# A two-step norm of queries and keys, stores on another queue, and a moved output-gate pair in a hybrid decoder layer

## The chip, the cores and the metric

The kernel runs on one core of a Trainium2 chip. The core has TensorE (PE, matmuls; its weight loads are listed as PEld), VectorE (DVE), ScalarE (ACT), GpSimd (POOL) and SyncE (SP), each with an instruction queue of its own that is worked in order, and 16 DMA engines. The metric is the device time of one execution in microseconds (us); lower is better.

## What is computed

One decoder layer, sequence 1024, width 1024, in float32: a half-step SwiGLU feed-forward, a token mixer, and a second half-step feed-forward, each behind an RMS norm with a shift and a scale. The change lies in the mixer's input projections. Cut to them:

```python
u = h @ w_in
da_q, da_k, da_v, ml_qk, ml_v, ml_o, ml_i, ml_f = jnp.split(u, IN_SPLITS, axis=-1)
q = partial_rope(rmsnorm(da_q per 64 channels, g_qnorm), cos, sin)   # and k likewise
y_da = diff_attention(q, k, da_v, ...)
ml_qk = silu(causal_conv(ml_qk, conv_w, conv_b))                     # 4 taps
y_ml = mlstm(ml_q, ml_k, ml_v, ml_o, ...)                            # gated by sigmoid(ml_o)
return concatenate([y_da, y_ml]) @ w_out
```

## The kernel before

All activations lie transposed, channels on the 128 partitions, 512 positions (half the sequence) on the free axis. A large projection is done by pairs of 128-channel output tiles. For each pair `wino` (line 226) computes the two tiles over both halves of the sequence with seven products in place of eight (Strassen's scheme): the activations' quarters and their differences are named B11, B21, B22 and T1 to T4, and the weight sums are formed in `wsum`. A product is four blocks of three matmuls (`mm3`, lines 199 to 201), because every float32 operand is split into a rounded part and a rest. For each product `split_w` (lines 187, 188) casts a weight block on ScalarE and takes the rest on VectorE. Results are added on VectorE (line 229).

A planner orders the instructions of each engine when the kernel is built: it simulates the engines and takes, by the order of the program, what is ready in its simulation. Buffers of a pool are handed out in the order of the program, and an instruction that writes into a reused buffer waits for the last use of the old one, a store included. `keep_in_program_order`, which the change uses, fixes an instruction's place.

The mixer's projections run in this order: values of attention (`wdv`, two pairs), gates, first mLSTM value pair (`wmv` 0), four pairs of queries and keys (`wqk`, `qk_handlers`), second mLSTM value pair (`wmv` 1), four pairs for the convolutions (`wcv`, `conv_handlers`), two pairs of output gates (`wmo`, `o_handlers`). Then mLSTM and attention heads follow.

What is left to do for a pair is put into `L.pending` and called by `late` in a later pair, behind its product T1. That holds for the transposes of values (line 642) and for `qk_finish` (line 591). `qk_finish` is called once for the queries and once for the keys: eight small matmuls sum the squares of each group of 64 channels (line 598), VectorE takes the reciprocal root (lines 601, 602), ScalarE spreads it into a tile `c` per half of the sequence (line 605), four matmuls turn that tile (line 609), ScalarE copies it back (line 611), and `qk_turned` scales, rotates and splits the four tiles of that half (lines 614 to 631). Each split tile is stored to DRAM in two parts (`qkd`, line 631, SP's queue). The raw tiles lie in eight buffers `qraw`, the casts in three buffers `qhi`. The queries and keys are in the pool `qkp`; when it closes, the convolutions' pool `cvp` takes the same memory, so the first write into `cu` (memset, line 726, or copy, line 746) waits for the last store out of `qkp`.

Other stores of the mixer, all on SP's queue: attention values (line 1136), mLSTM values (1141), convolved queries and keys (739), gates (758). GpSimd's queue carries attention's loads (lines 765 to 772). The first mLSTM head's loads stand on ScalarE's queue (lines 859 to 861); the buffer of the third lies where the gates' tiles lay.

Of the kernel before, what the change touches and what calls it, by code (L numbers as in the profile page):

```python
# [25 lines left out]
P = 128  # L26
# [104 lines left out]
HALF = [slice(0, HT), slice(HT, T)]  # L131


class Layer:
    def __init__(self, tc, A, es):
        self.tc, self.nc, self.A, self.es = tc, tc.nc, A, es
        nc = self.nc
        pool = lambda name, **k: es.enter_context(tc.tile_pool(name=name, **k))
        self.const = pool("const", bufs=1)
        c = self.const  # L140
        self.ones = c.tile([P, 1], F32, name="ones")
        nc.vector.memset(self.ones, 1.0)
        self.eps = c.tile([P, 1], F32, name="eps")
        nc.vector.memset(self.eps, EPS)
        self.mod = c.tile([P, 72], F32, name="mod")
        self.G = c.tile([P, 24], F32, name="G")
        self.gate = c.tile([P, 24], F32, name="gate")
        self.bada = c.tile([P, 72], F32, name="bada")
        self.gn = c.tile([P, 24], F32, name="gn")
        self.cs = c.tile([P, KT], F32, name="cs")  # L150
        self.B, self.full = {}, {}
        self.nct = 3
        self.sums = nc.gpsimd
        self.pending = []

    def ps(self):
        return self.mmps.tile([P, HT], F32, tag="mm", name="mm")
# [4 lines left out]
    def late(self):  # L162

        p, self.pending = self.pending, []
        for f in p:
            f()

# [58 lines left out]
    def wino(self, src, got11, out, got, st=None):  # L226
# [6 lines left out]
        if st is None:  # L233
# [18 lines left out]
            c22 = out("22")  # L252
            add(c22, w, y7)
            self.prod(z3, self.split_w(self.wsum(a12, s2, ALU.subtract)), "B22", True)
        else:
            p1 = st["p1"]
            s1 = self.wsum(a21, a22, ALU.add)
# [333 lines left out]
    def qk_finish(self, which):  # L591

        nc = self.nc
        ps = self.ps()
        for hf in range(2):
            for i in range(4):
                c = 8 * (4 * hf + i)
                nc.tensor.matmul(ps[:, c:c + 8], self.accs[which][hf][:, i * P:(i + 1) * P], self.bd[:, 0:P:16],
                                 start=True, stop=True, skip_group_check=True)
        v, y, t = (self.qkp.tile([P, 64], F32, tag=f"qn{i}", name=f"qn{i}") for i in range(3))  # L600
        nc.vector.tensor_scalar(out=v, in0=ps[:, 0:64], scalar1=1.0 / 64, scalar2=EPS, op0=ALU.mult, op1=ALU.add)
        self.rsqrt(y, t, v)
        for hf in range(2):
            r = self.ct()
            nc.scalar.copy(out=r.rearrange("p (c d) -> p c d", d=16),
                           in_=y[:, 32 * hf:32 * hf + 32].unsqueeze(2).broadcast_to([P, 32, 16]))
            ps = self.ps()
            for i in range(4):
                nc.tensor.matmul(ps[:, i * P:(i + 1) * P], r[:, i * P:(i + 1) * P], self.ident,
                                 start=True, stop=True, skip_group_check=True)  # L610
            nc.scalar.copy(out=r, in_=ps)
            self.qk_turned(which, hf, r)

    def qk_turned(self, which, hf, r):
        nc = self.nc
        hs = HALF[hf]
        for t in range(4):
# [10 lines left out]
            nc.scalar.copy(out=hi, in_=x)  # L628
            nc.vector.tensor_tensor(out=x, in0=x, in1=hi.bitcast(F32), op=ALU.subtract)
            for part, src in ((0, hi.bitcast(F32)), (1, x)):  # L630
                nc.sync.dma_start(out=self.qkd[which][:, part, 16 * t:16 * t + 16, hs], in_=src)


    def v_handlers(self, store):
# [85 lines left out]
    def conv_handlers(self, h):  # L720
# [2 lines left out]
        us = []  # L723
        for i in range(2):
            u = self.cvp.tile([P, T + 3], F32, tag="cu", name="cu", bufs=4)
            nc.gpsimd.memset(u[:, 0:3], 0.0)
            us.append(u)
        place = {"12": (0, 1), "21": (1, 0), "22": (1, 1)}
        at = lambda e, hf: us[e][:, 3 + hf * HT:3 + (hf + 1) * HT]
# [1 line left out]
        def conv(e):  # L731
# [4 lines left out]
            for j in range(1, 4):  # L736
                nc.vector.scalar_tensor_tensor(out=v, in0=u[:, j:j + T], scalar=cw(j), in1=v, op0=ALU.mult, op1=ALU.add)
            nc.scalar.activation(out=v, in_=v, func=AF.Silu)
            nc.sync.dma_start(out=self.mlqk[i], in_=v)

        def got(n, c):
            if n == "12":
# [5 lines left out]
    def o_handlers(self, pr):  # L748

        nc = self.nc  # L750
        t = lambda n=None: self.mle.tile([P, HT], F32, tag="vc", name="vc", bufs=6)
        place = {"12": (0, 1), "21": (1, 0), "22": (1, 1)}

        def fin(e, hf, src, v):
            h = 2 * pr + e
            nc.scalar.activation(out=v, in_=src, func=AF.Tanh, scale=0.5)
            nc.vector.tensor_scalar(out=v, in0=v, scalar1=1.0, scalar2=self.ghalf[:, h:h + 1], op0=ALU.add, op1=ALU.mult)
            nc.sync.dma_start(out=self.mlo[h][:, HALF[hf]], in_=v)
        return (lambda x: fin(0, 0, x, t())), t, lambda n, c: fin(*place[n], c, c)


# [210 lines left out]
def build(tc, yT, **A):  # L972
    nc = tc.nc
    with ExitStack() as es:
# [158 lines left out]

        def dav_store(pr):
            def store(e, hf, v):
                nc.sync.dma_start(out=davd[:, 4 * hf:4 * hf + 4, 2 * pr + e, :], in_=v)
            return store

        def mlv_store(pr):
            def store(e, hf, v):  # L1140
                nc.sync.dma_start(out=L.mlv[2 * pr + e][:, 4 * hf:4 * hf + 4, :], in_=v)
            return store
        dvh = [L.v_handlers(dav_store(pr)) for pr in range(2)]
        starts = [L.wino_p1(A["wdv"][i]) for i in range(2)]
# [63 lines left out]
        for which in range(2):  # L1208
# [11 lines left out]
                    L.wino(A["wqk"][i], seen11, out, got)  # L1220
            L.pending.append(lambda w=which: L.qk_finish(w))
        L.wino(A["wmv"][1], *L.v_handlers(mlv_store(1)))
        pq.close()

        pq, qpool = stack("right")
        L.cvp = qpool("cvp", bufs=2)
        for h in range(4):
            L.wino(A["wcv"][h], *L.conv_handlers(h))
        for pr in range(2):
            L.wino(A["wmo"][pr], *L.o_handlers(pr))  # L1230
        pq.close()
        pm.close()
        pt.close()
# [132 lines left out]
```

## Time and profile before

| | us |
|---|---|
| median of 3 runs | 2032.3 |
| lowest and highest | 2028.05, 2034.02 |
| profiled execution | 2026.9 |
| its span, first to last instruction | 2025.1 |
| PE busy in the span | 1919.7 (95%) |
| DVE busy | 1472.3 (73%) |
| ACT busy | 775.0 (38%) |
| POOL busy | 279.5 (14%) |

The first feed-forward fills the span until about 700 us, the mixer's projections lie between about 740 and 1082 us, mLSTM and attention between 1082 and 1220, the output projection and the second feed-forward behind. In the profile a time in brackets behind an instruction is the time for which its engine stood idle ahead of it, with what ended that. PEclk is the granted clock of TensorE as a share of its full 2.4 GHz; 0.50 is the lower level, 1.2 GHz. Busy times of neighbouring instructions overlap a little.

### The profile page before, as it was taken

To read this page: it belongs to the slowest core of one execution; us is meant where nothing else is said; L and a number is where in the kernel's file an instruction comes from. 1 tells how busy PE (TensorE), PEld (TensorE's weight loads), DVE (VectorE), ACT (ScalarE), POOL (GpSimd) and SP (SyncE) were. 2 spreads that over 40 slices of the span, in tenths; PEclk is the share of its full clock that TensorE was granted. 3 is DMA by queue.
4 is the path that set the end of the run, shared out by engine and by line. 5 is a ranking of instruction groups with operands and counts; after the bars stand their busy time and mean duration, and the time that the engine had idled before them with its cause. 6 is when DMAs were issued, how large, how long until landed. Compare 5 with 4: busy or idle time off the path is not lost.

```text
span 2025.1 us, 24549 instructions
## 1 busy us (share of the span) xinstructions
PE 1919.7 (95%) x8870; PEld 1583.3 (78%) x8870; DVE 1472.3 (73%) x2605; ACT 775.0 (38%) x1494; POOL 279.5 (14%) x225
## 2 busy tenths in 40 slices
PE   4999999999999988989998988999999999999999
PEld 3778888888888876877787867877888888888887
DVE  8998888777766689578785986479766655656665
ACT  4622232222232366334455866255222232222232
POOL 0111212211121100000001001004212111121120
PEclk8999999999999999989998999999999999999999
DMA  8343333222221242223439853121111111111113
GB/s 303 129 142 136 119 120 105 85 82 104 101 72 58 94 148 75 77 101 127 148 117 224 172 120 115 53 84 63 63 63 42 63 63 42 51 54 53 53 63 125
DMA packets 83274, 202.82 MB, mean 100 GB/s; under 512 B 9680, under 2 KB 18256, under 8 KB 83152
## 3 DMA queue, kind: packets, MB, share of 16 engines
q1 hardware_dynamic: 77504, 184.93, 26.8%
q0 software_dynamic: 4320, 14.75, 3.9%
q8 instruction: 70, 1.15, 0.2%
q10 hardware_dynamic: 1328, 1.57, 0.2%
q14 instruction: 52, 0.43, 0.1%
HBM read 174.02 MB, written 27.26 MB: 99 GB/s over the span
## 4 chain that ended last, share of the span: by engine, by line
PE 79%; DVE 9%; DMA 6%; ACT 2%; issue 2%; POOL 1%; SPq 0%; ACTq 0%; DVEq 0%; POOLq 0%
PE mm L199 25%; PE mm L200 25%; PE mm L201 25%; DMA ok<-qkd 2%; DMA qkd<-qhi 1%; DVE S L378 1%; DVE adaacc L324 1%; PE t L817 1%; POOL sf L194 1%; DVE wlo L188 1%; DVE S L420 1%; DMA adac<-in_wada 1%; DMA wraw<-in_w 1%; DVE S L429 1%; DMA qkd<-qraw 1%
## 5 line engine op out<-in xcount | busy, mean ns | idle before, releaser
L187 ACT CAST whi<-wraw 128x512 fp32r<-128x512 f32 x308 | 190.8, 621 | 476.1 <-PE mm L200 440.3
L199 PE MATMUL mm<-S,whi 128*128 128x512 f32 x900 | 353.4, 393 | 7.0 <-ACT whi L187 3.6
L200 PE MATMUL mm<-S,whi 128*128 128x512 f32 x900 | 352.5, 392 | 0.0
L201 PE MATMUL mm<-S,wlo 128*128 128x512 f32 x900 | 351.9, 392 | 0.0
L529 DVE SCALAR_TENSOR_TENSOR x<-mm,gate,x 128x512 f32<-128x512 f32 x368 | 269.6, 745 | 94.1 <-PE mm L201 93.2
L187 ACT CAST whi<-sf 128x512 fp32r<-128x512 f32 x224 | 138.9, 621 | 412.1 <-PE mm L200 387.3
L188 DVE TENSOR_TENSOR wlo<-wraw,whi 128x512 fp32r<-128x512 f32 x300 | 211.7, 707 | 87.9 <-ACT whi L187 75.8
L200 PE MATMUL mm<-glo,whi 128*128 128x512 f32 x672 | 261.8, 390 | 0.0
L201 PE MATMUL mm<-ghi,wlo 128*128 128x512 f32 x672 | 260.8, 391 | 0.0
L199 PE MATMUL mm<-ghi,whi 128*128 128x512 f32 x672 | 260.2, 392 | 0.1
L194 POOL TENSOR_TENSOR sf<-wraw 128x512 f32<-128x512 f32 x84 | 125.1, 1489 | 593.5 <-DMA wraw<-in_w 454.4
L199 PEld LDWEIGHTS mm<-S,whi 128*128 128x128 f32 x900 | 170.7, 190 | 44.1 <-ACT whi L187 4.5
L201 PEld LDWEIGHTS mm<-S,wlo 128*128 128x128 f32 x900 | 170.3, 189 | 36.2 <-DVE wlo L188 0.6
L200 PEld LDWEIGHTS mm<-S,whi 128*128 128x128 f32 x900 | 170.2, 189 | 35.0
L188 DVE TENSOR_TENSOR wlo<-sf,whi 128x512 fp32r<-128x512 f32 x224 | 156.9, 701 | 40.6 <-ACT whi L187 40.3
L199 PEld LDWEIGHTS mm<-ghi,whi 128*128 128x128 f32 x672 | 126.6, 189 | 26.4 <-ACT ghi L522 0.6
L201 PEld LDWEIGHTS mm<-ghi,wlo 128*128 128x128 f32 x672 | 126.6, 188 | 26.3
L200 PEld LDWEIGHTS mm<-glo,whi 128*128 128x128 f32 x672 | 126.6, 188 | 26.1
L229 DVE TENSOR_TENSOR c<-w,mm 128x512 f32<-128x512 f32 x84 | 57.3, 687 | 99.5 <-PE mm L201 99.4
L194 POOL TENSOR_TENSOR sf<-wraw,sf 128x512 f32<-128x512 f32 x42 | 64.2, 1527 | 442.1 <-DVE wlo L188 354.1
L324 DVE SCALAR_TENSOR_TENSOR adaacc<-adac,cs,adaacc 128x256 f32<-128x256 f32 x196 | 110.3, 563 | 12.6 <-DMA adac<-in_wada 11.4
L199 PE MATMUL mm<-B11h,whi 128*128 128x512 f32 x248 | 100.1, 411 | 9.4 <-ACT B11h L383 7.2
(332 smaller groups left out, 3387.7 us busy)
## 6 DMA issues: line engine op xcount, KB each, us to landing
wraw<-in_w SPq DMA_DIRECT2D x142, 512.0 KB
adac<-in_wada SPq DMA_DIRECT2D x112, 256.0 KB
ok<-qkd POOLq DMA_DIRECT2D x16, 512.0 KB, 12.2
adaraw<-in_wada SPq DMA_DIRECT2D x12, 512.0 KB
wraw<-in_wo SPq DMA_DIRECT2D x12, 512.0 KB
x<-in_xT SPq DMA_DIRECT2D x16, 256.0 KB
xd<-x SPq DMA_DIRECT2D x16, 256.0 KB
wraw<-in_wqk SPq DMA_DIRECT2D x8, 512.0 KB
```

The lines of the kernel that those rows point to most:

```text
L187: nc.scalar.copy(out=hi, in_=raw)
L188: (eng or nc.vector).tensor_tensor(out=lo, in0=raw, in1=hi.bitcast(F32), op=ALU.subtract)
L194: self.sums.tensor_tensor(out=s, in0=a, in1=b, op=op)
L199: nc.tensor.matmul(ps, whi, xhi, start=first, stop=False, skip_group_check=True)
L200: nc.tensor.matmul(ps, whi, xlo, start=False, stop=False, skip_group_check=True)
L201: nc.tensor.matmul(ps, wlo, xhi, start=False, stop=last, skip_group_check=True)
L229: add = lambda o, a, b: nc.vector.tensor_tensor(out=o, in0=a, in1=b, op=ALU.add)
L324: nc.vector.scalar_tensor_tensor(out=acc, in0=raws[k], scalar=self.cs[:, k:k + 1], in1=acc, op0=ALU.mult, op1=ALU.add)
L378: eng.tensor_tensor(out=h, in0=x, in1=r, op=ALU.mult)
L420: eng.tensor_tensor(out=o, in0=a, in1=b, op=ALU.subtract)
L429: e.tensor_tensor(out=T[n][1], in0=v, in1=T[n][0].bitcast(F32), op=ALU.subtract)
L529: self.nc.vector.scalar_tensor_tensor(out=x, in0=ps, scalar=self.gate[:, g:g + 1], in1=x, op0=ALU.mult, op1=ALU.add)
```

## The change

`qk_finish` is cut in two: sums, root and spreading stay where they were; turning, copying back and `qk_turned` become a closure that `later` calls behind product B22 of the same pair, two products further on, with the turning matmuls kept in program order. The stores of queries and keys, convolutions, gates and both kinds of values go from SP's queue to GpSimd's. The memset of the first three columns of `cu` goes from GpSimd to VectorE. The first output-gate pair is computed ahead of the convolutions, while the pool of queries and keys is still open.

```diff
-        self.pending = []
+        self.pending, self.after_t3 = [], []
...
+    def later(self):
+
+        p, self.after_t3 = self.after_t3, []
+        for f in p:
+            f()
...
             self.prod(z3, self.split_w(self.wsum(a12, s2, ALU.subtract)), "B22", True)
+            self.later()
...
+        rs = []
         for hf in range(2):
             r = self.ct()
             nc.scalar.copy(out=r.rearrange("p (c d) -> p c d", d=16),
                            in_=y[:, 32 * hf:32 * hf + 32].unsqueeze(2).broadcast_to([P, 32, 16]))
-            ps = self.ps()
-            for i in range(4):
-                nc.tensor.matmul(ps[:, i * P:(i + 1) * P], r[:, i * P:(i + 1) * P], self.ident,
-                                 start=True, stop=True, skip_group_check=True)
-            nc.scalar.copy(out=r, in_=ps)
-            self.qk_turned(which, hf, r)
+            rs.append(r)
+
+        def turn():
+            for hf, r in enumerate(rs):
+                ps = self.ps()
+                for i in range(4):
+                    self.tc.keep_in_program_order(
+                        nc.tensor.matmul(ps[:, i * P:(i + 1) * P], r[:, i * P:(i + 1) * P], self.ident,
+                                         start=True, stop=True, skip_group_check=True))
+                nc.scalar.copy(out=r, in_=ps)
+                self.qk_turned(which, hf, r)
+        self.after_t3.append(turn)
...
-                nc.sync.dma_start(out=self.qkd[which][:, part, 16 * t:16 * t + 16, hs], in_=src)
+                nc.gpsimd.dma_start(out=self.qkd[which][:, part, 16 * t:16 * t + 16, hs], in_=src)
...
-            nc.gpsimd.memset(u[:, 0:3], 0.0)
+            nc.vector.memset(u[:, 0:3], 0.0)
...
-            nc.sync.dma_start(out=self.mlqk[i], in_=v)
+            nc.gpsimd.dma_start(out=self.mlqk[i], in_=v)
...
-            nc.sync.dma_start(out=self.mlo[h][:, HALF[hf]], in_=v)
+            nc.gpsimd.dma_start(out=self.mlo[h][:, HALF[hf]], in_=v)
...
-                nc.sync.dma_start(out=davd[:, 4 * hf:4 * hf + 4, 2 * pr + e, :], in_=v)
+                nc.gpsimd.dma_start(out=davd[:, 4 * hf:4 * hf + 4, 2 * pr + e, :], in_=v)
...
-                nc.sync.dma_start(out=L.mlv[2 * pr + e][:, 4 * hf:4 * hf + 4, :], in_=v)
+                nc.gpsimd.dma_start(out=L.mlv[2 * pr + e][:, 4 * hf:4 * hf + 4, :], in_=v)
...
         L.wino(A["wmv"][1], *L.v_handlers(mlv_store(1)))
+        L.wino(A["wmo"][0], *L.o_handlers(0))
         pq.close()
...
         for h in range(4):
             L.wino(A["wcv"][h], *L.conv_handlers(h))
-        for pr in range(2):
-            L.wino(A["wmo"][pr], *L.o_handlers(pr))
+        L.wino(A["wmo"][1], *L.o_handlers(1))
```

## Rows read from the trace of the kernel before

**Rows 1.** Windows: busy us (count) of each engine, PEclk, DMA share, GB/s.
```profile
886.00:899.90 13.90, 8.56 (x39) 7.59 (x40) 9.19 (x23) 3.85 (x7) 0.00 (x0) 0.65 0.30 94
899.90:939.80 39.90, 39.25 (x172) 31.01 (x171) 33.15 (x56) 18.49 (x33) 0.00 (x0) 1.00 0.39 133
939.80:951.40 11.60, 7.31 (x35) 6.30 (x35) 7.54 (x21) 3.10 (x6) 0.00 (x0) 0.71 0.32 113
...
977.50:986.00 8.50, 3.94 (x13) 3.18 (x13) 3.11 (x5) 3.82 (x6) 0.33 (x4) 0.80 0.61 216
986.00:1056.00 70.00, 70.00 (x311) 57.93 (x310) 64.88 (x84) 36.47 (x50) 0.40 (x4) 1.00 0.28 102
1056.00:1082.00 26.00, 25.70 (x115) 20.75 (x113) 13.13 (x22) 9.54 (x15) 4.62 (x9) 1.00 0.87 193
1082.00:1099.00 17.00, 10.13 (x43) 8.08 (x44) 5.59 (x16) 6.32 (x22) 0.00 (x0) 0.60 0.89 293
```

**Rows 2.** Waits of PE from 740 to 1100: total us, times, longest.
```profile
PE mm L609 <- ACT c L605: 9.1, 4, 3.5
...
PE modps L642 <- ACT vt L644: 5.2, 2, 4.6
```

**Rows 3.** Timeline of PE, first norm: start, us, instruction, [idle before, releaser].
```profile
886.57 1.95 PE L598 MATMUL mm<-bd,k 128*128 128x8 f32 x16 [0.76 <-DVE k L587]
892.05 2.07 PE L609 MATMUL mm<-ident,c 128*128 128x128 f32 x8 [3.53 <-ACT c L605]
...
901.42 0.39 PE L199 MATMUL mm<-B22h,whi 128*128 128x512 f32 x1
...
904.16 0.39 PE L199 MATMUL mm<-B11h,whi 128*128 128x512 f32 x1
...
915.28 0.50 PE L199 MATMUL mm<-S,whi 128*128 128x512 f32 x1
```

**Rows 4.** Timeline of PE, second norm and the stop before the convolutions.
```profile
940.59 0.64 PE L642 MATMUL modps<-ident,vc 128*128 128x128 f32 x4
944.26 1.74 PE L609 MATMUL mm<-ident,c 128*128 128x128 f32 x8 [3.04 <-ACT c L605]
...
952.98 0.39 PE L199 MATMUL mm<-B22h,whi 128*128 128x512 f32 x1
...
982.23 1.12 PE L642 MATMUL modps<-ident,vc 128*128 128x128 f32 x4 [4.56 <-ACT vt L644]
983.00 0.78 PE L199 MATMUL mm<-S,whi 128*128 128x512 f32 x1
...
985.68 0.40 PE L199 MATMUL mm<-S,whi 128*128 128x512 f32 x1
```

**Rows 5.** Timelines of DVE and ACT: three waits for stores.
```profile
914.54 0.69 DVE L229 TENSOR_TENSOR qraw<-w,mm 128x512 f32<-128x512 f32 x1 [4.26 <-DMA qkd<-qraw]
...
981.11 0.59 ACT L746 COPY cu<-mm 128x512 f32<-128x512 f32 x1 [9.34 <-DMA qkd<-qraw]
...
1085.99 1.28 ACT L876 ACT_TABLE_LOAD   x1 [3.98 <-DMA mlo<-vc]
```

**Rows 6.** Timelines of POOL and SP: a memset, attention's loads, the last gate stores.
```profile
981.35 0.51 POOL L726 MEMSET cu<- 128x3 f32 x4 [223.18 <-DMA qkd<-qraw]
...
1061.20 0.91 POOL L765 DMA_DIRECT2D dav<-davd  x1 [43.64 <-PE mm L201]
...
1073.15 0.59 POOL L772 DMA_DIRECT2D ok<-qkd  x1
...
1079.84 3.04 SPq L758 DMA_DIRECT2D mlo<-vc  x2
```

**Rows 7.** DMA issues: count, KB each, median us from issue to landing.
```profile
ok<-qkd POOLq DMA_DIRECT2D x16, 512.0 KB, 12.2
...
maskqb<-in_maskq POOLq DMA_DIRECT2D x1, 32.0 KB, 2.2
```

**Rows 8.** Windows of 2 us: weight loads alone, then stores of turned tiles.
```profile
928.00:930.00 2.00, 2.00 (x9) 1.42 (x8) 1.92 (x4) 0.91 (x2) 0.00 (x0) 1.00 0.89 283
...
964.00:966.00 2.00, 2.00 (x11) 1.65 (x10) 2.00 (x4) 0.00 (x0) 0.00 (x0) 1.00 0.53 202
```

## The prediction

> **What bounds the kernel now.** I read the windows by stage first, then the waits of TensorE, then the timelines around the longest of them. The windows [rows 1] cover the mixer's projections, where all of the change lies. In the convolution stretch (986 to 1056 us) PE is busy for 70.00 of 70.00 us at clock 1.00: TensorE sets the pace, and VectorE keeps up at 64.88 of 70. Around the two norms of queries and keys (886 to 899.9 and 939.8 to 951.4) PE is busy for 8.56 of 13.90 and 7.31 of 11.60 us at a mean clock of 0.65 and 0.71, so it stands still and then works partly at the lower of its two levels (1.2 GHz). Before the convolutions (977.5 to 986) it is busy for 3.94 of 8.50 us. At the change to attention (1082 to 1099) it has 10.13 of 17.00 us. The waits name the causes [rows 2]: the turning matmuls (line 609) wait 9.1 us for the spread reciprocal roots, and a transpose (line 642) waits 5.2 us for ScalarE. The timelines [rows 3, 4] place these. Since PE is what every stretch waits for here, a microsecond of PE stop taken away is a microsecond of the time, as long as nothing else comes last in its place.
>
> **Part 1, the norm in two steps.** Price of a product (12 matmuls): from 901.42 to 904.16 is 2.74 us at full clock [rows 3]. First norm: the column sums end at 886.57 + 1.95 = 888.52, and the products T3 and B22 behind the turning are done at 904.16, so 15.64 us pass [rows 3]. The work in them is two products, 5.48, and two groups of turning matmuls. One group takes 2.07 us at the low clock, so about 1.03 at the full one, and 2.06 for both. That leaves 15.64 - 7.54 = 8.1 us as the most that can be won. T3 and B22 cover the chain from column sums to spread roots, which now costs 3.53 us of stop [rows 3]: 5.48 us of cover, 2 to spare. What comes late next: line 229 writes the next pair's results into the eight qraw buffers, and at 914.54 it waits 4.26 us for a store of a turned tile; that pair's T4 on PE starts only at 915.28, right behind it [rows 3, 5]. The first turned group now ends at 888.52 + 5.48 + 1.03 = 895.0 instead of 894.1, so with a chain of unchanged length T4 starts at 916.2. PE can do the two products that now follow T4 ahead of it (seven PSUM buffers hold the open results of two pairs), so the gain is 5.48 - 0.9 = 4.6. Bounds: 8.1 if the stores get quicker by 3.5 us or more, -0.9 if the planner does not let those products run ahead. I take 4.6, the value for stores as they are now.
>
> Second norm: from 940.59 + 0.64 = 941.23 to the start of B22 at 952.98 are 11.75 us [rows 4]; T3 and both turning groups need 2.74 + 2.06, so 6.9 us go. Here no matmul soon after needs a buffer of the turned tiles, so I take all of it.
>
> VectorE's part: over both stretches of the first norm (886 to 939.8) it is busy for 9.19 + 33.15 = 42.3 of 53.8 us [rows 1]. With 4.6 us taken out it is at 86%, with 8.1 at 93%, which is the density at which it feeds PE without loss in the convolutions (64.88 of 70). No price.
>
> **Part 2, an output-gate pair ahead.** Seven products, 19.2 us of PE, move from behind the convolutions to ahead of them; they need none of the queries' and keys' buffers. Now ScalarE's copy into cu waits 9.34 us for the last store of a turned tile and goes on at 981.11 [rows 5]; behind it in ScalarE's queue stand the copy of a transposed tile and the weight casts, so PE stops for 4.56 us until 982.23 and works at the low clock until 985.68 [rows 4]. The loss is 4.56, 0.4 for the slow transpose, and 985.68 - 983.00 less six matmuls of 0.228, 1.3: together 6.3 us. Cover: turning ends one slow T3 ahead of 952.98, at about 949.0, and from there to the stop at 977.67 PE has ten products (T3, and nine in 24.7 us). It will have ten less two plus seven, 41 us, against 32 us from turning to the last landing (949.0 to 981.1). The stop goes; 9 us are to spare. Behind the convolutions one pair is left as cover for the last convolution's taps, and in the stretch of the last gate pair VectorE is busy for only 13.13 of 26 us [rows 1]: no price. Should the cover fail, the 6.3 us return.
>
> **Part 3, stores by GpSimd's queue and memsets on VectorE.** 64 stores (32 of queries and keys, 8 each of the two value kinds, of convolutions and of gates) leave SP's queue. At 0.59 us each, as the loads on that queue [rows 6], they occupy GpSimd for 38 us of some 340, and it is nearly idle there (POOL column, rows 1). SP's weight loads no longer stand behind stores, but no PE wait there names a late load, so nothing is won. Eight memsets of about 0.13 us [rows 6] go to VectorE: 1 us in its 5 us of room per 70. What changes is the landing. No store lies on this queue today. The nearest rows are a 32 KB load that lands after 2.2 us and 512 KB loads, seven in a row, at a median of 12.2 [rows 7]. I take a store alone to land near the small one, about 1 us later than SP's last gate store, which is issued at about 1082.6 and has landed at the latest when ScalarE goes on at 1085.99, 3.4 us later. That store lies on the path: ScalarE's third load of the first mLSTM head waits for it 3.98 us, with attention's exponentials behind it [rows 5, 6]. So +1.0, bounds 0 (landing as now) and +8.8 (12.2 less 3.4).
>
> While the turned tiles are stored, the DMA engines are at a share of 0.53 with 202 GB/s; weights alone reach 0.89 with 283 [rows 8]. It looks as if about half of the engines carry these stores and the rest stand idle. The Trainium skill (DMA: Bandwidth & Descriptors, "Why a DMA increments its semaphore by 16 and not by 1") says that a copy uses the largest number of engines up to 16 that divides the slowest dimensions of both sides, always the lowest-numbered from SP's queue, but consecutive ones from a moving cursor on GpSimd's. The slowest dimension of qkd here is 8, and the share agrees; that neighbouring stores would take opposite halves no row shows. By the rule part 1 would be worth 8.1 and not 4.6. Against the change speaks another page (SBUF - State Buffer, "Who interferes with whom"): VectorE in a two-port mode locks GpSimd out while it writes descriptors. That page excepts tensor_tensor, the bulk here, and the GpSimd loads beside a working VectorE show issues of 0.59 us [rows 6], so I give it no price.
>
> **Sum.** -4.6 - 6.9 - 6.3 + 1.0 = -16.8 us against the profiled execution, 2026.9 us (span 2025.1 and 1.8 around it): 2010.1. The runs' median, 2032.3, is 5.4 above the profiled execution, so 2015.5 is the forecast for the median, with 2010 to 2021 as its own range (part 1 between 8.1 and about 2, VectorE lagging by up to 3).
>
> **The rivals.** (a) *PE bound throughout, quicker stores.* If neighbouring stores use both halves of the engines, the sixteen stores of a norm (4.2 MB, 21 us at 202 GB/s) need about half that time, VectorE's 4.26 us wait goes, and T4 never waits: -8.1 - 6.9 - 6.3 + 0 = -21.3, 2011. For it: the share of 0.53. Against it: a single store isn't shortened by this. This is the case of the DMA page. (b) *The release wait moves to VectorE.* The memsets into cu wait for the same landing as ScalarE's copy, and VectorE is in order: if the planner places them early, weight splits stand behind them. Price up to the 9.34 us that ScalarE waits now, say 8: 2023. For it: GpSimd's first memset waited 223 us there [rows 6]; against it: 19.2 us of cover. (c) *Attention's first loads behind stores.* Seven loads leave GpSimd from 1061.20 to 1073.74, and PE's first scores come right behind their landing. Placed behind the last gate store (1082.6), the last of them would leave at 1082.9 + 7 x 0.59 = 1087, 13 us later, and attention starts as much later: -16.8 + 13 = -3.8, 2028. Against it: gate stores are ready late, loads early. (d) *Slow landing on GpSimd's queue, slower than before.* Every store takes the 12.2 us of the loads. With three cast buffers the eight tiles of a norm go in three rounds, 3 x 12.2 + 7.5 = 44 us instead of 32. The pair behind the first norm waits for the last of them: +6.5 there in place of -4.6. -6.9 stays; the stop before the convolutions returns by 3 (44 against 41), so -3.3; the last gate store costs +8.8: +5.1, and with the transposed value tiles, which wait on two buffers, about +8 by my estimate, 2040. It decides from a landing of about 10 us. Against it: 12.2 holds for 3.5 MB in a row. (e) *The change does not do what it says:* PE is not let ahead of T4, part 1 gives -0.9 instead of a gain: 2021.
>
> **How the numbers follow.** Forecast 0.40, (a) 0.24, (b) 0.12, (c) 0.11, (d) 0.09, (e) 0.04. A measurement of this kernel tells 0.3%, 6.1 us, from no change. Faster by more: forecast, a, b, e = 0.80; within: c = 0.11; slower: d = 0.09. The range takes all but (d) and the outer ends: from 2005 (case a, with 6 us for a planner's order that falls better elsewhere; the waits of line 609 and 642 alone are 14.3) to 2030 (case c). Predicted is the likeliest case, 2015.
>
> **What would show it.** Line 609 with no idle ahead of it and clock 1.00 from 886 to the convolutions; the wait of line 642 gone, the copy into cu without a DMA wait; VectorE's wait on a qkd store at line 229 as long as now (forecast) or gone (a); memsets of line 726 with a wait on VectorE (b); attention loads issued behind the last gate store (c); qkd stores with a landing above 10 us (d). Wrong would be the whole if PE stops anew behind the first turning.

## The result, and the profile after

| | before | after |
|---|---|---|
| median of 7 runs, us | 2029.33 | 2043.38 |
| lowest and highest, us | 2024.08, 2034.02 | 2038.48, 2049.85 |
| ratio, 95% interval | | 1.0077 [1.0064, 1.0091] |
| span of the profiled execution, us | 2025.1 | 2041.6 |

The changed kernel is slower by 0.77%, some 15.6 us of 2030; forecast were 16.8 us less. In the changed file the lines stand 6 to 14 numbers further down: the products are L205 to L207 (before L199 to L201), the casts and rests L193 and L194, the results L235, column sums L605, turning L622, scaling L634, rotation L637 to L640, split and stores L642, L643 and L645, the copy into cu L760, its memset L740, gate stores L772, convolution stores L753, attention's loads L779 to L786, first scores L804.

First the windows by stage, as [rows 1]: the two stretches of the first norm, the second norm's column sums and what follows, the stretch before the convolutions, 70 us of convolutions and gates, and the change to attention.

```profile
core 0: us, PE busy (x) PEld busy (x) DVE busy (x) ACT busy (x) POOL busy (x), PEclk, DMA share, GB/s
885.00:898.40 13.40, 12.90 (x73) 11.29 (x74) 9.65 (x23) 5.96 (x11) 0.54 (x1) 1.00 0.29 99
898.40:942.00 43.60, 32.14 (x133) 25.85 (x131) 31.52 (x53) 17.08 (x31) 9.62 (x16) 0.84 0.45 133
942.00:955.00 13.00, 11.59 (x49) 10.07 (x50) 6.48 (x19) 2.79 (x5) 0.60 (x1) 0.74 0.21 62
1000.00:1015.00 15.00, 7.95 (x28) 6.11 (x27) 5.13 (x12) 2.85 (x4) 0.00 (x0) 0.79 0.23 81
1015.00:1085.00 70.00, 69.87 (x308) 57.25 (x307) 62.58 (x84) 36.00 (x48) 6.97 (x13) 1.00 0.29 107
1085.00:1111.00 26.00, 0.40 (x2) 0.43 (x2) 0.57 (x1) 2.60 (x6) 4.25 (x9) 0.54 1.19 260
```

The first norm itself is mended: PE busy for 12.90 of 13.40 us at clock 1.00, where it was 8.56 of 13.90 at 0.65 [rows 1]. The loss has moved: 11 us are idle in the stretch behind, 7 in the one before the convolutions, and at the change to attention PE is busy for 0.40 of 26 us, where it had 25.70 of 26 and then 10.13 of 17 [rows 1]. PE's waits from 740 to 1111, as [rows 2], give the names of the three largest:

```profile
PE s L804 <- DMA ok<-qkd: 25.7, 1, 25.7
PE mm L205 <- DVE qraw L235: 10.7, 1, 10.7
PE mm L207 <- DVE wlo L194: 7.1, 1, 7.1
```

The wait of the turning matmuls (9.1 us before) is no longer in the list, and that of the transpose has gone from 5.2 to 0.7. The timeline of PE, as [rows 3, 4]:

```profile
885.50 1.95 PE L605 MATMUL mm<-bd,k 128*128 128x8 f32 x16 [0.76 <-DVE k L594]
...
892.87 1.95 PE L622 MATMUL mm<-ident,c 128*128 128x128 f32 x16
...
910.76 0.39 PE L207 MATMUL mm<-B22h,wlo 128*128 128x512 f32 x1
921.87 0.79 PE L205 MATMUL mm<-S,whi 128*128 128x512 f32 x1 [10.72 <-DVE qraw L235]
...
927.02 0.40 PE L205 MATMUL mm<-B11h,whi 128*128 128x512 f32 x1
...
1011.17 0.79 PE L207 MATMUL mm<-B21h,wlo 128*128 128x512 f32 x1 [7.05 <-DVE wlo L194]
...
1110.60 0.66 PE L804 MATMUL s<-ok,oq 128*128 128x128 f32 x2 [25.73 <-DMA ok<-qkd]
```

*Stop 1, T4 of the pair behind the first norm.* PE does two products ahead of T4, as the prediction had it, and then stands from 911.15 to 921.87. VectorE and ScalarE show why (their timelines, as [rows 5]):

```profile
907.51 0.62 ACT L642 CAST qhi<-vc 128x512 fp32r<-128x512 f32 x1 [0.91 <-DVE vc L640]
...
913.84 0.62 ACT L642 CAST qhi<-qraw 128x512 fp32r<-128x512 f32 x1 [2.21 <-DMA qkd<-qhi]
...
921.13 0.69 DVE L235 TENSOR_TENSOR qraw<-w,mm 128x512 f32<-128x512 f32 x1 [0.36 <-DMA qkd<-qraw]
...
971.32 1.65 ACT L642 CAST qhi<-qraw 128x512 fp32r<-128x512 f32 x3
...
1009.82 0.69 DVE L200 TENSOR_TENSOR sf<-wraw 128x512 f32<-128x512 f32 x1 [12.43 <-DMA wraw<-in_wcv]
...
1010.22 0.58 ACT L760 COPY cu<-mm 128x512 f32<-128x512 f32 x1 [11.07 <-DMA qkd<-qraw]
...
1010.43 0.69 DVE L194 TENSOR_TENSOR wlo<-wraw,whi 128x512 fp32r<-128x512 f32 x1
```

The turning ends at 894.8 and the first cast begins at 907.51, 12.7 us later. Before, the first group ended at 894.1 and the first cast began at 902.84, 8.7 us later. From then on the casts wait for the stores of their three buffers, and the result that T4 waits for is written at 921.13. Counted from the column sums that is 35.6 us, before 28.0 [rows 3, 5]. The delay goes on to the second norm: its column sums wait 2.1 us more for the squares of the late results, and the product behind them runs at the lower clock (the row from 942, mean clock 0.74).

*Stop 2, before the convolutions.* The second turning ends at 956.0, its first cast follows at 971.32, the last store leaves at 997.00, and ScalarE's copy into cu goes on at 1010.22: 54 us from turning to release where the prediction set 32 against a cover of 41. PE found 48 us of work there (956.0 to 1004.1). What it stops for is not that copy, though: it is a rest of a weight block (L194, 1010.43) that stands in VectorE's queue behind a weight sum, and the sum waits 12.43 us for the weights of the second convolution pair. That load left SP's queue at 995.20 and landed 14.5 us later, at 1009.7, where loads of these weights land after 3.9 at the median. So the last store and a weight load arrive within 1 us of each other, and the prediction had only the store. By the order in ScalarE's queue PE would otherwise have come up against the copy within a product, since the cast of the next product's weights begins behind it at 1010.70; no run separates the two here.

*Stop 3, the first scores.* The timeline of GpSimd, as [rows 6]:

```profile
997.00 0.61 POOL L645 DMA_DIRECT2D qkd<-qraw  x1 [1.72 <-DMA mlo<-vc]
...
1083.29 0.55 POOL L772 DMA_DIRECT2D mlo<-vc  x1 [1.96 <-DVE vc L771]
1084.00 0.91 POOL L779 DMA_DIRECT2D dav<-davd  x1 [0.17 <-PE mm L207]
...
1087.26 0.61 POOL L785 DMA_DIRECT2D ok<-qkd  x1
1089.96 0.59 POOL L786 DMA_DIRECT2D ok<-qkd  x1 [2.08 <-DMA mlo<-vc]
1093.72 0.60 POOL L772 DMA_DIRECT2D mlo<-vc  x1 [3.17 <-DMA mk<-mlqk]
```

Attention's seven loads leave from 1084.00 to 1089.96, right behind the third gate store of that pair, which waits for VectorE's gate. Before, they left from 1061.20 [rows 6], 21 us ahead of the first scores at 1082.64. The scores go on with the landing of the sixth load (1087.26). It left 14.7 us later than before (1072.57) and took 23.2 us to land where it took 9.9, together the 28.0 us by which the scores are late. The landings from 740 to 1130, as [rows 7] (KB each, median us from issue to landing; the keys' loads are at 11.1 before in the same window):

```profile
qkd<-qhi POOLq DMA_DIRECT2D x16, 256.0 KB, 7.3
mlqk<-cv POOLq DMA_DIRECT2D x8, 512.0 KB, 2.9
ok<-qkd POOLq DMA_DIRECT2D x8, 512.0 KB, 17.6
qkd<-qraw POOLq DMA_DIRECT2D x15, 256.0 KB, 10.1
mlo<-vc POOLq DMA_DIRECT2D x8, 256.0 KB, 9.2
```

Not all of stop 3 reaches the end. From the first scores to the first product of the second feed-forward the two kernels need (windows, before and after):

```profile
1082.64:1347.52 264.88, 238.61 (x1466) 201.12 (x1467) 190.92 (x490) 164.38 (x482) 24.73 (x34) 0.97 0.49 124
```

```profile
1110.60:1362.85 252.25, 236.48 (x1467) 199.68 (x1467) 193.00 (x490) 161.68 (x478) 25.31 (x34) 0.98 0.46 113
```

PE's idle time in this stretch falls from 26.3 to 15.8 us: behind the first scores its waits for exponentials go from 10.1 to 4.3 us and those for keys from 7.7 to 4.4. That these got done while PE stood is the likely reason; no run shows it by itself. So the account of the two profiles closes: first column-sum matmul to first scores 196.1 before and 225.1 after, +29.0; to the second feed-forward -12.6; ahead of it -1.1 and behind +1.2; together +16.5, the difference of the spans.

### The profile page after: what moved, and what is told of

The parts are those of the page before. It is cut to its first block, busy times and chain, and to the rows that moved or that the text cites. A ratio compares the mean times of both kernels' runs of the same rounds, so it can differ in the third digit from the quotient of the medians.

```text
span 2041.6 us, 24536 instructions
## 1 busy us (share of the span) xinstructions
PE 1916.4 (94%) x8870; PEld 1581.3 (77%) x8870; DVE 1476.8 (72%) x2613; ACT 773.6 (38%) x1494; POOL 313.2 (15%) x281
## 4 chain that ended last, share of the span: by engine, by line
PE 81%; DVE 8%; DMA 6%; ACT 3%; issue 2%; POOL 1%; SPq 0%; DVEq 0%; ACTq 0%; POOLq 0%
PE mm L205 25%; PE mm L206 25%; PE mm L207 25%; DMA ok<-qkd 3%; DVE adaacc L331 1%; DVE wlo L194 1%; DVE S L385 1%; PE t L831 1%; DMA adac<-in_wada 1%; DMA wraw<-in_wcv 1%; ACT S L387 1%; DVE S L436 1%; DVE nm L808 1%; POOL sf L200 1%; DMA qkd<-qraw 0%
## 5 line engine op out<-in xcount | busy, mean ns | idle before, releaser
L193 ACT CAST whi<-wraw 128x512 fp32r<-128x512 f32 x308 | 191.0, 622 | 476.9 <-PE mm L206 444.6
L205 PE MATMUL mm<-S,whi 128*128 128x512 f32 x900 | 354.4, 394 | 15.3 <-DVE qraw L235 10.7
L207 PE MATMUL mm<-S,wlo 128*128 128x512 f32 x900 | 352.2, 392 | 0.1
L193 ACT CAST whi<-sf 128x512 fp32r<-128x512 f32 x224 | 139.1, 621 | 414.6 <-PE mm L206 384.4
L194 DVE TENSOR_TENSOR wlo<-wraw,whi 128x512 fp32r<-128x512 f32 x300 | 210.4, 703 | 87.6 <-ACT whi L193 74.7
L207 PE MATMUL mm<-ghi,wlo 128*128 128x512 f32 x672 | 260.4, 390 | 0.0
L205 PE MATMUL mm<-ghi,whi 128*128 128x512 f32 x672 | 259.9, 391 | 0.1
L200 POOL TENSOR_TENSOR sf<-wraw 128x512 f32<-128x512 f32 x84 | 120.9, 1439 | 600.0 <-DMA wraw<-in_w 436.7
L205 PEld LDWEIGHTS mm<-S,whi 128*128 128x128 f32 x900 | 170.6, 190 | 52.7 <-DVE qraw L235 11.3
L207 PEld LDWEIGHTS mm<-S,wlo 128*128 128x128 f32 x900 | 170.4, 189 | 36.4 <-DVE wlo L194 1.0
L194 DVE TENSOR_TENSOR wlo<-sf,whi 128x512 fp32r<-128x512 f32 x224 | 158.5, 707 | 37.2 <-ACT whi L193 36.9
L205 PEld LDWEIGHTS mm<-ghi,whi 128*128 128x128 f32 x672 | 126.3, 188 | 26.3 <-ACT ghi L529 0.6
L207 PEld LDWEIGHTS mm<-ghi,wlo 128*128 128x128 f32 x672 | 126.3, 188 | 26.1
L235 DVE TENSOR_TENSOR c<-w,mm 128x512 f32<-128x512 f32 x84 | 57.2, 686 | 98.7 <-PE mm L207 98.6
L205 PE MATMUL mm<-B11h,whi 128*128 128x512 f32 x248 | 100.3, 412 | 10.3 <-ACT B11h L390 7.1
```

The costliest lines, as they stand in the source:

```text
L193: nc.scalar.copy(out=hi, in_=raw)
L194: (eng or nc.vector).tensor_tensor(out=lo, in0=raw, in1=hi.bitcast(F32), op=ALU.subtract)
L200: self.sums.tensor_tensor(out=s, in0=a, in1=b, op=op)
L205: nc.tensor.matmul(ps, whi, xhi, start=first, stop=False, skip_group_check=True)
L207: nc.tensor.matmul(ps, wlo, xhi, start=False, stop=last, skip_group_check=True)
L235: add = lambda o, a, b: nc.vector.tensor_tensor(out=o, in0=a, in1=b, op=ALU.add)
```

## The experiments

The measure beside the ratio is the stretch from the first column-sum matmul to the first scores, short "the stretch" (196.1 us before, 225.1 after). Each kernel is one profile there, and a profiled execution can lie some 6 us from the median of its kernel (2041.25 against 2034.97 in one case), so ratios decide.

**Gate stores back on SP.**

```diff
-            nc.gpsimd.dma_start(out=self.mlo[h][:, HALF[hf]], in_=v)
+            nc.sync.dma_start(out=self.mlo[h][:, HALF[hf]], in_=v)
```

> The changed kernel with the gate stores alone back on SP's queue. Theory L (the loss comes from attention's first seven loads, which stand behind gate stores in GpSimd's queue): the loads leave as soon as their buffers are free, about 20 us before the projections end, PE's stop of 25.7 us before the first scores shrinks to under 5 us, and the time falls by 15 to 25 us, to at or below the kernel before. Theory S (the loss comes from the slow landing of the query and key stores on GpSimd's queue, stops of 10.7 and 7.1 us): both of those stops stay, and the time falls by less than 8 us.

Ratio 1.0056 [1.0034, 1.0078], 2042.8 us; the stretch 216.9. The stop before the scores falls to 16.3 only. GpSimd shows what now stands ahead:

```profile
1079.19 0.53 POOL L753 DMA_DIRECT2D mlqk<-cv  x1 [7.35 <-ACT cv L752]
1079.97 0.93 POOL L779 DMA_DIRECT2D dav<-davd  x1 [0.25 <-PE mm L207]
```

It is the last convolution store, which waits for its Silu. Theory L misses its numbers: the stop does not go, and the time falls by 0.0021 or 4 us, not by 15 to 25. Theory S keeps its own, as the two other stops stay (12.0 and 6.5); the next run speaks against it. Which store it is doesn't matter: the loads leave behind whatever late store has been put ahead of them.

**Query and key stores back on SP.**

```diff
-                nc.gpsimd.dma_start(out=self.qkd[which][:, part, 16 * t:16 * t + 16, hs], in_=src)
+                nc.sync.dma_start(out=self.qkd[which][:, part, 16 * t:16 * t + 16, hs], in_=src)
```

> The changed kernel with the query and key stores alone back on SP's queue. Theory S: the stop of 10.7 us behind the first turning and that of 7.1 us in the first convolution pair go, with the low clock behind them, and the time falls by 12 to 20 us. Theory L: the stop of 25.7 us before the first scores stays, and the time stays above the kernel before.

Ratio 1.0087 [1.0067, 1.0107], the stretch 224.6. Stop 1 shrinks to 7.9 and stop 2 to waits of 2.0 and 1.3, stop 3 is 26.8. Some 3 us of stop 1 thus come with these stores on GpSimd's queue. But the wait at the second norm's column sums grows by 2.0, and the time doesn't gain, as theory L expected: these stores are not what makes the change slow.

**All stores and the memset as before; norm and order as changed.**

All five kinds of stores are edited like the one shown.

```diff
-            nc.gpsimd.dma_start(out=self.mlqk[i], in_=v)
+            nc.sync.dma_start(out=self.mlqk[i], in_=v)
...
-            nc.vector.memset(u[:, 0:3], 0.0)
+            nc.gpsimd.memset(u[:, 0:3], 0.0)
```

> Parts 1 and 2 of the change without part 3: all stores on SP's queue, the memsets on GpSimd. If the prediction's steps for parts 1 and 2 hold, 16 to 21 us less than the kernel before (ratio 0.990 to 0.992). If the new order of the planner costs by itself (VectorE does all eight scalings of the turned tiles ahead of the first rotation, so the first casts come 5 us later), the stop behind the first turning stays at several us and the gain is under 10 us.

Ratio 1.0026 [1.0016, 1.0035], the stretch 204.3. Stop 3 is gone (1.0 us), stops 1 and 2 stay with 7.9 and 9.8. So two thirds of the loss come with the stores, and the rest of the change still doesn't win.

**Only the stores and the memset changed.** The mirror of the last: norm and order as before.

> The kernel before with part 3 alone: all mixer stores on GpSimd's queue and the memsets on VectorE. Theories L and S together: attention's first loads behind the gate stores, +20 to +28 us, and longer stops for the query and key stores, +5 to +10 us: ratio 1.012 to 1.019. If part 3 costs only in combination with the new order, within 0.3% of before.

Ratio 1.0031 [1.0021, 1.0040], the stretch 211.3. PE's waits from 860 to 1100:

```profile
PE s L790 <- DMA ok<-qkd: 21.1, 1, 21.1
PE mm L609 <- ACT c L605: 9.1, 4, 3.5
```

Stop 3 is there without the other parts. The loss, 6.3 us, lies far below the 25 to 38 expected (1.012 to 1.019), and at the edge of the 0.3% of the other line. The stop of 4.56 us before the convolutions is gone without the moved pair: PE waits 0.4 us there. The release did not come earlier for it: the copy into cu goes on 33.1 us behind the second turning (950.16), before 31.8. But in ScalarE's new order the copy of a transposed tile stands ahead of the copy into cu, where before it stood behind (981.59):

```profile
974.50 0.59 ACT L644 COPY vt<-modps 128x512 f32<-128x512 f32 x1 [0.23 <-PE modps L642]
...
983.26 0.59 ACT L746 COPY cu<-mm 128x512 f32<-128x512 f32 x1 [5.09 <-DMA wraw<-in_wcv]
```

**Only the norm in two steps.**

```diff
-        self.pending = []
+        self.pending, self.after_t3 = [], []
...
+            self.later()
...
+        self.after_t3.append(turn)
```

> The kernel before with part 1 alone (norm in two steps). The prediction's step says -11.5 us (4.6 and 6.9). Theory C (the chain from turning to the first stored tile has grown, because both halves' turned tiles now come at once and VectorE scales all eight before it rotates the first, and the casts queue behind the rotated tile): the stops at the turning go, but a stop of about 8 us ahead of T4 of the pair behind the first norm and a longer one before the convolutions take their place, and the time is within 6 us of the kernel before.

Ratio 1.0046 [1.0032, 1.0060], the stretch 205.6: the part that was to win 11.5 us loses 9.3. PE waits 8.0 us for T4 and 11.0 before the convolutions, the two stops that the expectation named; the time lies beyond its 6 us.

**The same, with one half turned behind T3 and the other behind B22.**

Each call of `later` now takes one closure, and it is called behind T3 too.

```diff
-        def turn():
-            for hf, r in enumerate(rs):
+        def turn(hf):
...
-        self.after_t3.append(turn)
+        self.after_t3 += [lambda: turn(0), lambda: turn(1)]
...
+            self.later()
             c22 = out("22")
             add(c22, w, y7)
```

> Part 1 alone, but the first half is turned behind T3 and only the second behind B22, so that the halves come one product apart as before. Theory C: the first cast comes about 8 us behind the first turning instead of 13, the stop ahead of T4 falls from 8 to under 4 us, and the time is 4 to 8 us under that of part 1 alone. Theory D (VectorE has simply no room in this stretch, whatever the order): the stop ahead of T4 stays within 2 us of that of part 1 alone.

Ratio 1.0008 [0.9994, 1.0022], the stretch 195.4, 10.2 less than with both halves together. The first cast of each, both halves together and split:

```profile
911.82 0.62 ACT L642 CAST qhi<-vc 128x512 fp32r<-128x512 f32 x1 [0.91 <-DVE vc L640]
```

```profile
907.60 0.62 ACT L642 CAST qhi<-vc 128x512 fp32r<-128x512 f32 x1 [0.24 <-DVE vc L640]
```

From the column sums (889.83 and 891.19) that is 22.0 and 16.4 us; before it was 16.3. The stop at T4 falls from 8.0 to 1.5, with the same work on VectorE; of the 11.0 us before the convolutions 6.0 stay. That speaks for a longer chain and against a VectorE that has no room. Of the 5.6 us by which the first cast comes sooner, 3.8 are a shorter chain: from ScalarE's copy of the first turned tile (L624) to the first cast pass 9.7 us in place of 13.5, and 8.6 before. The rest is that the first half is turned one product earlier. For this norm, in the kernel with both halves together, VectorE's order holds all eight scalings (L634) ahead of the rotation, and the three unrotated casts of a half stand behind the rotated one in ScalarE's queue.

**Only the moved output-gate pair.**

```diff
         L.wino(A["wmv"][1], *L.v_handlers(mlv_store(1)))
+        L.wino(A["wmo"][0], *L.o_handlers(0))
```

> The kernel before with part 2 alone (first output-gate pair ahead of the convolutions, all stores on SP's queue). The prediction's step: the stop of 4.56 us before the convolutions and the low clock behind it go, -6.3 us. If the planner places the copies into cu so that ScalarE waits for the stores all the same (theory W), the stop comes again 19 us later and the time is within 3 us of before.

Ratio 0.9975 [0.9962, 0.9988], the stretch 190.0, 6.1 less than before. The copy into cu goes through without a wait, and the transpose's stop is gone from PE's waits. This is what the prediction's step expected, and not theory W:

```profile
989.85 0.58 ACT L746 COPY cu<-mm 128x512 f32<-128x512 f32 x1
```

**Only the query and key stores on GpSimd's queue,** the rest as before.

> The kernel before with the 32 query and key stores alone on GpSimd's queue. If they land earlier there as a group (neighbouring stores on different engines), the stop before the convolutions goes and nothing stands ahead of attention's loads: -5 to -9 us. If their landing on this queue is slower in sum (theory S), the stop before the convolutions and the wait ahead of T4 grow, +3 to +10 us.

Ratio 1.0000 [0.9985, 1.0014], the stretch 193.4. The stop before the convolutions goes down to two of about 1.1 us, in the same new order on ScalarE as above. What it gives there doesn't show in the time, so neither expectation holds, a gain of 5 to 9 us or a loss of 3 to 10.

**The change with gate and convolution stores back on SP.** The edit of the first experiment and the same for the stores of line 753.

> The changed kernel with the stores of gates and of convolutions both back on SP's queue; the other stores stay on GpSimd's, norm and order as changed. Theory L (attention's seven loads stand in GpSimd's in-order queue behind stores that wait for late results; putting the gates back alone did not free them, since then the last convolution store stood ahead): now no late store stands ahead of them. They leave from about 1055 to 1068, as in the kernel with the moved output-gate pair alone, the first scores wait under 5 us for the keys in place of 25.7 and 16.3, and from the first column-sum matmul to the first scores pass about 225.1 - 22 = 203 us (gates alone: 216.9). Time 2043 - 20 = 2023, ratio to before about 0.997. The stops of 10.7 (T4) and some 6 us (before the convolutions) stay as they are. Rival (the loads are slow in themselves, 14 to 18 us at landing, because the stores on the same queue keep the DMA engines busy): the loads leave early, but PE still stops over 10 us for the keys; time 2036 or more.

Ratio 1.0025 [1.0012, 1.0039], the stretch 202.0 (203 expected). The loads leave from 1070.65 and the scores hardly wait for them:

```profile
1070.65 0.93 POOL L779 DMA_DIRECT2D dav<-davd  x1 [70.53 <-PE mm L206]
```

```profile
1092.54 0.41 PE L804 MATMUL s<-ok,oq 128*128 128x128 f32 x2 [2.06 <-DMA ok<-qkd]
```

So stop 3 is the order in GpSimd's queue, and the loads are not slow in themselves: the sixth lands after 10.8 us here, after 23.2 in the change. The time falls by 10.6 us (0.0052 of 2030) and not by the expected 20: part of the 23.1 us was given back behind the scores anyway.

**The same, and the turning split by halves.**

> As the kernel with gates and convolutions on SP's queue, and the turning cut by halves: the half-0 tile is turned behind T3, the half-1 tile behind B22, so that VectorE gets the first four tiles one product earlier and the halves don't come together. If the two causes found (attention's loads behind late stores, and the lengthened chain from turning to the first cast) are all that makes the change slow, they add: the step from the first column-sum matmul to the first scores falls by about 20 for the first and by about 9 for the second (10.2 between the two kernels that hold the norm alone), to 225.1 - 29 = 196 or less, and with the moved gate pair's 6 us against before to some 193; time 2029 - 3 to - 8, 2021 to 2026, ratio 0.996 to 0.999. If a third cost of the same size is hidden in the queries' and keys' stores on GpSimd's queue, the T4 stop stays above 5 us and the sum above 200; time 2033 or more.

Ratio 0.9949 [0.9931, 0.9968], 2020.4 us, the stretch 186.8. PE's waits from 860 to 1111:

```profile
PE s L804 <- ACT e L810: 5.0, 1, 5.0
PE mm L204 <- DVE qraw L234: 3.2, 2, 2.3
PE mm L605 <- DVE k L594: 3.1, 2, 2.4
...
PE mm L206 <- DVE wlo L193: 1.5, 1, 1.5
```

With the two causes taken out and everything else of the change left in, the change is faster. The split gives 15.1 us of the stretch here against 10.2 alone, more than the sum: with the shorter chain the release before the convolutions also comes almost under the cover of the moved pair, where PE waits 1.5 us in place of 6.7.

**Moved pair, split norm, rotated tile last, all stores on SP.**

```diff
-        for t in range(4):
+        for t in (1, 2, 3, 0):
             x = self.raws[which][hf][t]
```

> The moved output-gate pair with the norm in two steps cut by halves, all stores on SP's queue, and of the four tiles of a half the rotated one last in place of first. If it is the length of the chain from turning to the casts that decides, casts that don't queue behind the rotated tile come about 2 us sooner (first cast at about 905 where the column sums start at 890), the stop before T4 goes below 1 us, and the sum of the split norm (-0.7) and the moved pair (-6.1) grows by 1 to 3: from the first column-sum matmul to the first scores about 187 us, time 2020 to 2022, ratio 0.995 to 0.997. Rival (the order of tiles only exchanges which buffer comes free last): as the sum, 189.5 or more, and time 2024 or more, no better than the moved pair alone (0.9975).

Ratio 0.9937 [0.9921, 0.9953], 2018.7 us, the stretch 186.4. The first cast follows the first turning group (891.62 + 1.16) by 1.5 us:

```profile
894.28 1.29 ACT L642 CAST qhi<-qraw 128x512 fp32r<-128x512 f32 x2 [0.82 <-DVE qraw L634]
```

T4 waits 0.8 us, and the copy into cu goes through without a wait; what is left are 4.9 us at the second norm's column sums and 1.8 for a weight cast in the moved pair. This is the fastest kernel of the study, ahead of both the kernel before and the changed one. Whether the order of the tiles helps isn't shown: no run has the moved pair and the split norm on SP's queue without it. The stretch is 2.9 us under the sum of the two parts (189.3), but the kernel of the experiment before, with the rotated tile first, is also under it (186.8), and its ratio is within the noise of this one.

**Moved pair, and query and key stores on GpSimd's queue.**

> The kernel before with the moved output-gate pair, and with the stores of queries and keys alone on GpSimd's queue. Those stores alone gave 193.4 us from the first column-sum matmul to the first scores and a ratio of 1.0000, the pair alone 190.0 and 0.9975; their gain was for the most part the same stop before the convolutions. If these stores land no sooner for T4 (7 to 10 us each), the two together give 189 to 190, time as with the pair alone, 0.997 to 0.998. If the second half of the DMA engines helps the buffers behind the first norm come free, VectorE's wait of 4.26 us at the results of the next pair falls below 2 and the time by as much: 2021 to 2022, 0.995 to 0.996.

Ratio 0.9992 [0.9978, 1.0006], the stretch 192.1: neither line of the expectation holds, 0.997 to 0.998 with a stretch of 189 to 190, or 0.995 to 0.996. The stores landed after 6.5 and 7.3 us at the median, and beside the moved pair, which removes the same stop, they bring nothing.

## Why the prediction was wrong, point by point

Three kernels give the account in time, as differences of their ratios (each ratio is known to about 0.0015, a difference to about 0.002 or 4 us) times 2030 us: taking the late loads away 0.0052 or 10.6 us, splitting the halves 0.0076 or 15.4 us, and what is left of the change is 0.0051 or 10.4 us faster than before. 10.6 + 15.4 - 10.4 = 15.6, the loss measured; the sum closes by its making, and what it shows is the size of each step.

*Part 1, first norm (-4.6).* The step that failed is "with a chain of unchanged length T4 starts at 916.2". The turning was won (no wait ahead of L622, clock 1.00), and PE did run two products ahead. But the chain got longer: in the kernel with this part alone T4 starts 33.7 us behind the first column-sum matmul (923.49 - 889.83) where 29.6 were set and 28.7 stood before. I moved the turning and kept the interval behind it from the old trace, in which the two halves came 3.3 us apart, and VectorE began to scale the first while the second was turned. With both halves ready at once, the order on VectorE and ScalarE is another, and the copy of the first turned tile is followed by the first cast after 13.5 us in place of 8.6. The lower bound of -0.9 had no room for this either, since it counted only PE's side.

*Part 1, second norm (-6.9).* "No matmul soon after needs a buffer of the turned tiles, so I take all of it" failed in the same way: the release for cu is such a use. With the norm alone it came at 1005.44, 44.5 us behind the turning (960.97), where it was 31.8; the stop before the convolutions grew from 4.56 to 11.0.

*Part 2 (-6.3).* Right in place and size when alone: -5.1 us by the ratio, -6.1 in the stretch. In the whole change it failed by its own condition, "should the cover fail": 54 us from turning to release against 41 of cover, and 48 of cover in fact. A second arrival that it did not count, the weight load that landed at 1009.7, held PE as well. The 9 us to spare were counted against a duration that part 1 itself lengthened; the two parts weren't independent, and I summed them as if they were.

*Part 3 (+1.0).* The step that failed is "that store lies on the path". The last gate store stands behind attention's loads in the queue, leaves at 1093.72 and lands 19.6 us later, beyond the 12.2 of the upper bound. ScalarE doesn't wait for it: the first mLSTM head's third load left at 1085.88, ahead of that store. The path leads through the seven loads, for which the sum had no term; they were rival (c).

*Rival (c), at 0.11, was the mechanism of the largest stop.* Its argument against ("gate stores are ready late, loads early") was the wrong way to read an in-order queue: the order is settled when the kernel is built, and a load that is ready waits behind a store that isn't. Its price of 13 us is near what the loads cost the time, 10.6, though by luck, two errors that cancel: the stop is 25.7 us, as the load that the scores wait for left 14.7 us later than before and took 13.3 us longer to land, which the price did not hold, and 12.6 us are given back behind the first scores. What I should have seen: this rival needs no bad luck, since the change puts stores that wait for the last projections into the very queue that carries the first loads of the next stage.

*Rival (b)* came up where stores went back to SP: with the gate stores there, and with gate and convolution stores, VectorE's memsets wait 9.29 and 9.81 us for a query or key store, and PE 6.5 and 6.7 for VectorE, near the price of 8. With the split turning that wait falls to 4.31, and PE's to 1.5. *Rival (d)* set its mark at 10 us of landing; the stores of queries and keys land after 7.3 and 10.1, so it lies at its edge. About 3 us of stop 1 come with these stores on GpSimd's queue: the stop is 10.7, 12.0 and 11.4 in the kernels that have them there and the norm in two unsplit steps, and 7.9, 7.9 and 8.0 in those with them on SP's. Whether that is their landing or their order in the queue is not shown. *Rival (a)* was half right. The changed kernel and the one with all stores on SP's queue, in the middle of stop 1 (windows, DMA share and GB/s last):

```profile
918.00:920.00 2.00, 0.00 (x0) 0.00 (x0) 0.00 (x0) 0.57 (x1) 0.00 (x0) 0.50 1.00 377
```

```profile
918.00:920.00 2.00, 0.00 (x0) 0.00 (x0) 0.93 (x2) 0.62 (x1) 0.00 (x0) 0.61 0.50 168
```

The share doubles, from 0.50 to 1.00, and the rate with it, and still T4 came no sooner (stops of 10.7 and 7.9 us): what T4 waits for is the end of a chain of casts and single stores. The rule of the Trainium skill (DMA: Bandwidth & Descriptors, "Why a DMA increments its semaphore by 16 and not by 1"), by which a copy that uses only some of the engines takes them from a moving cursor on GpSimd's queue and always the lowest-numbered on SP's, agrees with the shares; the gain that I worked out from it did not come.

What the forecast meant to win is there for the most part once both causes are out: those kernels come to -10.4 and -12.8 us where -16.8 was summed. They are kernels with the turning split, not the one that was forecast, and what is missing is not traced to the end.

## What to carry to other kernels

When work is moved, follow it to the release of its last buffer in the new order, and do not keep an interval from the old trace: here a product won ahead of a step was lost behind it, because two halves arrived together. Before a store is put on another engine's queue, list what stands behind it there, above all the loads that the next stage starts with; a store that waits for a late result holds them all. And a cover counted for one part of a change must be counted against the duration that the other parts leave.

## What was not expected of the hardware

While the last store of queries and keys and a weight load were on their way before the convolutions, nearly nothing moved: from 1006 to 1008 us the DMA engines were at a share of 0.07, about what one of the sixteen gives when it is busy throughout (1/16 is 0.06).

```profile
1006.00:1008.00 2.00, 0.00 (x0) 0.00 (x0) 0.00 (x0) 0.00 (x0) 0.00 (x0) 1.00 0.07 27
```

The last store left at 997.00 and what waited for it went on at 1010.22, 13 us later, while the convolution stores of twice the size landed after 2.9 at the median on the same queue. The weight load, on SP's queue, was as late. Why this tail is so slow no run here shows. TensorE's clock followed its stops: in the stop at T4 the granted clock fell to 0.50, its lower level of 1.2 GHz, and the twelve matmuls of T4 went at about 0.43 us each in place of 0.23, so that the stop cost PE 2.4 us more than its length (921.87 to 927.02 for a product of 2.74).
